# A layer chain on one core: the attention stage reordered into whole steps of two heads

## Chip, cores, metric

One Trainium2 chip, one of its cores. The kernel is one program in Bass with the Tile framework: the order of TensorE's instructions (PE) is the order in which the Python code issues them, while the orders of VectorE (DVE), ScalarE (ACT), GpSimd (POOL) and of the DMA queue on SyncE (SP) are set by Tile's scheduler, from the priorities that the code gives. Every engine then works through its own list strictly in that order and waits on semaphores. The metric is the time on the device in microseconds, a median over runs.

## What is computed

Two layers over 256 latent tokens and 256 context tokens of width 1024. Each layer is a half-step SwiGLU, a mixer (layer 0: neighbourhood attention, layer 1: a short gated convolution), and a second SwiGLU, each with an adaptive modulation and a LayerNorm. The stage that matters here is the attention of layer 0, with 16 heads of 64:

```python
qkv = (hx @ w_qkv).reshape(B, S, 3, N_HEADS, HEAD_DIM)
q = apply_axial_rope(qkv[:, :, 0], rope)
k = apply_axial_rope(qkv[:, :, 1], rope)
...
s_win = jnp.einsum('bjqhd,bjkhd->bhjqk', q_r, k_blk).astype(jnp.float32) * scale
s_win = jnp.where(mask, s_win + bias.astype(jnp.float32)[None], -jnp.inf)
s_ctx = jnp.einsum('bjqhd,bchd->bhjqc', q_r, k_c).astype(jnp.float32) * scale
p = jax.nn.softmax(jnp.concatenate([s_win, s_ctx], axis=-1), axis=-1).astype(v.dtype)
return (jnp.einsum('bhjqk,bjkhd->bjqhd', p[..., :nk], v_blk)
        + jnp.einsum('bhjqc,bchd->bjqhd', p[..., nk:], v_c))
...
y_lat = jnp.moveaxis(o, 0, 1).reshape(B, S, D) @ w_out
```

With 256 latent tokens in four grid rows, every query sees 256 latent keys (the window is a mask) and 256 context keys: 512 keys in all, four key tiles of 128.

## The kernel before

Everything is fp32, done as products of two parts: each operand is split into a high part `hi` (a copy by ACT) and a low part `lo` (a subtraction by DVE), and a product is hi·hi + hi·lo + lo·hi. So one pass over the contraction costs three matmuls, and whatever goes through TensorE is first touched once by ACT and once by DVE (`split`, lines 104-106).

**Weights.** `wunit` loads 256 rows by 512 columns by DMA (L175), then ACT makes `hi` in two halves (L178) and DVE `lo` in two halves (L181). There are four raw buffers, five for `hi` and five for `lo`; a buffer comes free when the last matmul that reads it is done.

**Chunks.** A chunk is the work on one token tile with one weight unit: six matmuls of 128x512 (L156, L157, L159). `tile_panel` makes a panel of four chunks for one token tile and hands the PSUM bank to `each`: for keys and values (`kv_quarter`, 256 columns of K and 256 of V, i.e. four heads), DVE applies the rotary factors to K (`roped`, L708 to L715; for context tokens ACT copies, L760) and `split` writes V. `q_half` makes Q for eight heads. After its panels, `rest` transposes K or Q on TensorE (kT, L773; qT, L791), and `split` makes the high and low parts. This `rest` is a `Late`: it runs when `tick`, called after every chunk, has counted its delay (1 chunk for kT, 2 for qT), or at once when somebody asks for it with `get()`.

**The attention pipeline.** `scores(h, qt)` takes two heads and one of the two query tiles: six matmuls S of 64x512 (L814) into two banks, then per head the bias (DVE L818), the maximum (DVE L820), the exponential (ACT L822), the reciprocal (DVE L823) and the scaling (ACT L824). `probs_T` transposes one head's 128x512 probabilities in four TensorE transposes (PT, L836) and splits them (ACT L105, DVE L106). When both query tiles of a head are there, `values(h)` multiplies with V: eight matmuls o of 128x256 (L848, L849), whose halves are added up (ACT L854, DVE L855) and, after the second head of a pair, split into `oT`. The loop runs over half-steps i, one head and query tile each: S of two heads at every even i, PT of one head two half-steps later (`A_LAG`), o of one head one half-step after that (`V_LAG`). Between them TensorE gets chunks from `fill`, at a rate per half-step (`R0` to `R3`): first the other quarters of K and V and the second half of Q (`filler`, 56 chunks), and from i = 24 on the first nine chunks of the output projection wo (`last_filler`), which need `oT`.

**PSUM.** Eight banks: three with tag `mm` (panels, o, two of wo's accumulators), three with tag `at` (S, and wo's third accumulator), two with tag `tp` (all transposes). Wo's accumulators are held from their first chunk until the attention is over, so that from then on one `mm` bank is left for o.

After the loop come the other wo chunks, the LayerNorm, and the next SwiGLU, whose weights are loaded ahead.

Of the kernel before, what the change touches and what calls it, by code (L numbers as in the profile page):

```python
# [35 lines left out]
LEAD = 5  # L36
TAIL = 3
XAT = 1
A_LAG = 2
A_PRE = 2  # L40
NX_AT = 2
R0 = 2.4
R1 = 2.9
R2 = 1.9
R3 = 1.0
LN_LAG = (5, 5)
LT_LAG = (5, 5)
F0_LAG = (5, 5, 6, 7)
G_LAG = 4
ROPE_EARLY = 70  # L50
S_EARLY = 40
V_LAG = 1
AHEAD = 3
P_EARLY = 70
V_EARLY = 70
W_HI = 2
# [8 lines left out]
def backbone_kernel(  # L65
# [315 lines left out]
    def run(gen):  # L381
        for _ in gen:
            pass
# [336 lines left out]
    def bias_pair(h, qt):  # L720


        for hh in (h, h + 1):
            bt = hp.tile([P, 4, 64], F32, tag="bias", bufs=4, name=nm("bias"))
            for i in range(2):
                bias_dma[:] = [sync.dma_start(bt[64 * i:64 * i + 64],
                                              bass.AP(na_rpb_rev.tensor,
                                                      na_rpb_rev.offset + hh * 465 + (7 - 2 * qt - i) * 31 - 48,
                                                      [[1, 64], [31, 4], [1, 64]]))]
            nc.gpsimd.tensor_tensor(out=bt, in0=bt, in1=win_sb[:, ::-1].unsqueeze(1).to_broadcast([P, 4, 64]),  # L730
                                    op=ALU.add)
            BIAS[hh, qt] = bt[:, :, ::-1]
# [71 lines left out]
    def scores(h, qt):  # L804

        ch = h % 8 // 2
        qh, ql = Q[h // 8].get()[ch // 2]
        qs = slice((ch % 2) * 256 + qt * P, (ch % 2) * 256 + (qt + 1) * P)
        kh, kl = KV[h // 4][0].get()[(h % 4) // 2]
        banks = [bank("at", "S") for _ in range(2)]  # L810
        for f in range(3):
            for i in range(2):
                ps = slice(64 * i, 64 * i + 64)
                nc.tensor.matmul(banks[i], (qh, qh, ql)[f][ps, qs], (kh, kl, kh)[f][ps, :], start=f == 0, stop=f == 2)  # L814
        res = []
        for i, S in enumerate(banks):
            Sv = S[:, 0:256].rearrange("p (a b) -> p a b", a=4)
            nc.vector.tensor_tensor(out=Sv, in0=Sv, in1=BIAS.pop((h + i, qt)), op=ALU.add)  # L818
            mx = hp.tile([P, 3], F32, tag="mx", bufs=6, name=nm("mx"))
            nc.vector.tensor_reduce(out=mx[:, 0:1], in_=S, axis=AX.X, op=ALU.max, negate=True)  # L820
            pr = hp.tile([P, 512], F32, tag="pr", bufs=4, name=nm("pr"))
            nc.scalar.activation(pr, S, AF.Exp, bias=mx[:, 0:1], accum_out=mx[:, 1:2])  # L822
            nc.vector.reciprocal(mx[:, 2:3], mx[:, 1:2])  # L823
            nc.scalar.activation(pr, pr, AF.Copy, scale=mx[:, 2:3])  # L824
            res.append(pr)
        return res
# [3 lines left out]
    def probs_T(h, qt, pr):  # L830
        if h not in PT:
            PT[h] = [hp.tile([P, 4, 256], F32R, tag="pt", bufs=4, name=nm("pT")) for _ in range(2)]
        pth, ptl = PT[h]
        pt = tpb("PT")
        for k in range(4):
            nc.tensor.transpose(pt[:, k * P:(k + 1) * P], pr[:, k * P:(k + 1) * P], ident)  # L836
        split(pt.rearrange("p (k q) -> p k q", k=4), pth[:, :, qt * P:(qt + 1) * P], ptl[:, :, qt * P:(qt + 1) * P])
# [3 lines left out]
    def values(h):  # L841

        pth, ptl = PT.pop(h)
        ps = mmb("o")[:, 0:256]
        s = slice(h % 4 * P, (h % 4 + 1) * P)
        v = KV[h // 4][1]
        for k in range(4):
            nc.tensor.matmul(ps, v[k][:, s], pth[:, k], start=k == 0, stop=False)  # L848
            nc.tensor.matmul(ps, v[k][:, s], ptl[:, k], start=False, stop=k == 3)  # L849
        if h % 2 == 0:  # L850
            osum[0] = sp.tile([P, 512], F32, tag="tmp", bufs=3, name=nm("osum"))[:, 0:256]
        p0 = h % 2 * 64
        t = osum[0][p0:p0 + 64]
        nc.scalar.activation(t, ps[64:128], AF.Copy)  # L854
        nc.vector.tensor_tensor(out=t, in0=ps[0:64], in1=t, op=ALU.add)  # L855
        if h % 2:
            if len(oT) <= h // 4:
                oT.append([hp.tile([P, 512], F32R, tag="oT", bufs=6, name=nm("oT")) if len(oT) < 3 else act(F32R, "oT")
                           for _ in range(2)])
            cs = slice((h // 2 % 2) * 256, (h // 2 % 2) * 256 + 256)  # L860
            split(osum[0], *(z[:, cs] for z in oT[h // 4]))
# [15 lines left out]
    def last_filler():  # L877
        with tc.issue_after(bias_dma[-1].ins):
            for t in range(2):
                for h in range(2):  # L880
                    xt[t][h] = act(F32, "x")
                    sync.dma_start(xt[t][h], xscr[t * P:(t + 1) * P, h * 512:(h + 1) * 512])
            gen, nh, lt = sub_end(na_w_out[0], lhs_T(oT), KC, 0, 1, 5, 1.0, (0, 6), "wo", order_late(KU))
        box.extend([nh, lt])
        yield from gen

    box = []
    fill = filler()
    rate = [R0] * 8 + [R1] * 8 + [R2] * 8 + [R3] * 12
    credit = 0.0  # L890
    steps = [(h + i, qt) for h in range(0, NH, 2) for qt in range(2) for i in range(2)]
    prs = {}
    LAG = A_LAG
    fin = None

    def fill_some(n):
        for _ in range(n):
            if next(fill, 0) == 0:
                break

    fill_some(A_PRE)
    for i in range(len(steps) + LAG + V_LAG):
        if i == NX_AT:
            new_x(0, 0, s2t)
            for t in range(2):
                for h in range(2):
                    sync.dma_start(xscr[t * P:(t + 1) * P, h * 512:(h + 1) * 512], xt[t][h])
        while i + AHEAD < len(steps) and len(KV) <= steps[i + AHEAD][0] // 4:
            fill_some(1)
        if i < len(steps) and i % 2 == 0:  # L910
            with tc.high_priority(offset=S_EARLY):
                prs[i], prs[i + 1] = scores(*steps[i])
            if i % 2 == 0 and i + 2 < len(steps):
                bias_pair(*steps[i + 2])
        credit += rate[min(i, len(rate) - 1)]
        n = int(credit)
        credit -= n
        if i >= 24 and fin is None:
            run(fill)
            fin = last_filler()  # L920
            fill = islice(fin, 9)
        fill_some((n + 1) // 2)
        if 0 <= i - LAG < len(steps):
            with tc.high_priority(offset=P_EARLY):
                probs_T(*steps[i - LAG], prs.pop(i - LAG))
        fill_some(n // 2)
        j = i - LAG - V_LAG
        if j >= 0 and steps[j][1] == 1:
            with tc.high_priority(offset=V_EARLY):
                values(steps[j][0])  # L930
    run(fill)
    run(fin)
    phase.__exit__(None, None, None)
# [129 lines left out]
```

## Time and profile before

| | us |
|---|---|
| median of 3 runs | 1285.99 (1285.16, 1285.99, 1287.23) |
| the profiled execution, its time | 1289.17 |
| its span in the profile | 1287.4 |
| attention loop, first S to last o | 441.8 to 589.3 |
| PE busy, whole span | 1257.7 (98%) |
| DVE / ACT busy, whole span | 955.1 (74%) / 591.2 (46%) |

The time of the profiled execution is 1.8 us more than its span. How to read the rows that follow: in the timeline a row has its start in us from the span's start, its length in us, the engine, the line, the operation, what it writes and reads, and the count where equal rows were merged; in brackets the time that the engine sat idle before it, and what ended the wait. In a view of stretches a row has the stretch, its length, and for PE, PEld (weight loads), DVE, ACT and POOL the busy time with the number of instructions, then TensorE's granted clock (1 is full), the share of the DMA engines' time, and GB/s. A matmul's length contains its way through the pipeline, so the time that one costs in a row of them is the distance between two starts.

### The profile page before, as it was taken

Reading aid. Unit: us, or ns where it says so; the run is one execution under the profiler, and the core shown is the slowest. Engines: PE = TensorE matmul, PEld = TensorE weight load, DVE = VectorE, ACT = ScalarE, POOL = GpSimd, SP = SyncE. Lnnn points to the kernel's source line nnn. Section 1 sums busy time; section 2 is a strip of 40 time slices with the busy share of each in tenths; the row PEclk is TensorE's granted clock in tenths of the full one; section 3 lists DMA queues with packets and bytes.
Section 4 is the critical chain, followed back from the end, with each engine's and each line's share of the span. In section 5 each row is a group of like instructions: output and inputs, shape, how many; then the busy total and the mean of one; then the engine's idle time right before and its main releaser. Section 6 shows DMA issues by size and latency. Waiting matters only on the chain.

```text
span 1287.4 us, 17193 instructions
## 1 busy us (share of the span) xinstructions
PE 1257.7 (98%) x5890; PEld 1007.0 (78%) x5890; DVE 955.1 (74%) x1683; ACT 591.2 (46%) x1148; POOL 42.0 (3%) x71
## 2 busy tenths in 40 slices
PE   7999999999999999988999999999999999999997
PEld 4787778788778877766887787887787877788886
DVE  3699877485658777788998787757778788855545
ACT  2432132413236456686555435654435645655431
POOL 0000000000001111110000000000000000000000
PEclk9999999999999999999999999999999999999999
DMA  9977569484622744464999887666887764666641
GB/s 284 299 231 243 181 193 297 131 297 146 198 78 76 215 91 92 90 147 149 305 331 328 295 294 262 215 215 225 289 287 241 215 211 147 210 217 185 231 155 51
DMA packets 202712, 268.59 MB, mean 209 GB/s; under 512 B 30026, under 2 KB 149298, under 8 KB 202624
## 3 DMA queue, kind: packets, MB, share of 16 engines
q1 hardware_dynamic: 202624, 267.49, 65.9%
q8 instruction: 46, 0.75, 0.2%
q14 instruction: 42, 0.34, 0.1%
HBM read 265.27 MB, written 2.17 MB: 208 GB/s over the span
## 4 chain that ended last, share of the span: by engine, by line
PE 78%; DVE 8%; DMA 8%; ACT 3%; issue 2%; SPq 1%; POOL 0%; DVEq 0%; ACTq 0%
PE w L156 13%; PE w L157 13%; PE w L159 13%; PE f L541 6%; PE f L542 6%; PE f L543 6%; DMA ar<-in_ada_w_dram 5%; DMA w1r<-in_ffn_w_in_dram 2%; PE wkv L156 2%; PE wkv L157 2%; PE wkv L159 2%; PE wc L156 2%; PE wc L157 2%; PE wc L159 2%; DVE w1l L181 2%
## 5 line engine op out<-in xcount | busy, mean ns | idle before, releaser
L178 ACT ACTIVATE w1h<-w1r 128x512 fp32r<-128x512 f32 x352 | 203.3, 626 | 185.0 <-PE w L159 75.4
L181 DVE TENSOR_TENSOR w1l<-w1r,w1h 128x512 fp32r<-128x512 f32 x352 | 227.6, 684 | 66.5 <-ACT w1h L178 64.3
L156 PE MATMUL w<-w1h,hTh 128*128 128x512 f32 x528 | 211.6, 401 | 3.8 <-ACT hTh L105 3.7
L247 DVE SCALAR_TENSOR_TENSOR acc<-ar,cst,acc 128x512 f32<-128x512 f32 x266 | 187.2, 745 | 34.8 <-DMA ar<-in_ada_w_dram 34.8
L157 PE MATMUL w<-w1l,hTh 128*128 128x512 f32 x528 | 207.7, 393 | 0.0
L156 PE MATMUL w<-w2h,gh 128*128 128x512 f32 (+1 forms) x446 | 175.4, 394 | 0.0
L157 PE MATMUL w<-w2l,gh 128*128 128x512 f32 (+1 forms) x446 | 173.7, 390 | 0.3 <-DVE w2l L181 0.3
L178 ACT ACTIVATE w2h<-w2r 128x512 fp32r<-128x512 f32 x176 | 101.5, 624 | 140.9 <-PE w L159 131.6
L159 PE MATMUL w<-w1h,hTl 128*128 128x512 f32 x528 | 163.9, 392 | 0.6 <-DVE hTl L106 0.6
L181 DVE TENSOR_TENSOR w2l<-w2r,w2h 128x512 fp32r<-128x512 f32 x176 | 114.0, 686 | 43.5 <-ACT w2h L178 42.3
L541 PE MATMUL f<-h0h,w1h 128*128 128x512 f32 x352 | 139.8, 397 | 0.4 <-ACT w1h L178 0.4
L542 PE MATMUL f<-h0h,w1l 128*128 128x512 f32 x352 | 138.4, 393 | 0.0
L543 PE MATMUL f<-h0l,w1h 128*128 128x512 f32 x352 | 138.3, 393 | 0.0
L159 PE MATMUL w<-w2h,gl 128*128 128x512 f32 (+1 forms) x446 | 136.3, 387 | 0.0
L156 PEld LDWEIGHTS w<-w1h,hTh 128*128 128x128 f32 x528 | 99.5, 188 | 28.2 <-ACT hTh L105 5.5
L159 PEld LDWEIGHTS w<-w1h,hTl 128*128 128x128 f32 x528 | 99.5, 189 | 24.1 <-DVE hTl L106 1.4
L157 PEld LDWEIGHTS w<-w1l,hTh 128*128 128x128 f32 x528 | 99.6, 189 | 20.4 <-DVE w1l L181 0.3
L156 PEld LDWEIGHTS w<-w2h,gh 128*128 128x128 f32 x446 | 83.7, 188 | 21.7 <-issue 1.7
L157 PEld LDWEIGHTS w<-w2l,gh 128*128 128x128 f32 x446 | 83.8, 188 | 18.6 <-DVE w2l L181 1.3
L159 PEld LDWEIGHTS w<-w2h,gl 128*128 128x128 f32 x446 | 83.3, 188 | 18.7
L541 PEld LDWEIGHTS f<-h0h,w1h 128*128 128x128 f32 x352 | 66.6, 189 | 18.4 <-issue 3.7
L543 PEld LDWEIGHTS f<-h0l,w1h 128*128 128x128 f32 x352 | 66.5, 189 | 14.7 <-DVE h0l L519 0.3
(178 smaller groups left out, 1702.5 us busy)
## 6 DMA issues: line engine op xcount, KB each, us to landing
w1r<-in_ffn_w_in_dram SPq DMA_DIRECT2D x352, 256.0 KB
ar<-in_ada_w_dram SPq DMA_DIRECT2D x128, 512.0 KB
w2r<-in_ffn_w_out_dram SPq DMA_DIRECT2D x88, 512.0 KB
ar<-in_ada_w_dram SPq DMA_DIRECT2D x32, 256.0 KB
wkvr<-in_na_w_qkv_dram SPq DMA_DIRECT2D x32, 256.0 KB
wcr<-in_sc_w_in_dram SPq DMA_DIRECT2D x32, 256.0 KB
wqr<-in_na_w_qkv_dram SPq DMA_DIRECT2D x8, 512.0 KB
bias<-in_na_rpb_dram SPq DMA_DIRECT2D x64, 64.0 KB
```

Of the source, the lines that this page charges most:

```text
L156: nc.tensor.matmul(ps, lh, rh, start=first and i == 0, stop=False)
L157: nc.tensor.matmul(ps, lh, rl, start=False, stop=False)
L159: nc.tensor.matmul(ps, ll, rh, start=False, stop=last and i == n - 1)
L178: nc.scalar.activation(hi[:, a:a + m // W_HI], raw[:, a:a + m // W_HI], AF.Copy)
L181: nc.vector.tensor_tensor(out=lo[:, a:b], in0=raw[:, a:b], in1=hi[:, a:b].bitcast(F32), op=ALU.subtract)
L247: nc.vector.scalar_tensor_tensor(out=a, in0=src, scalar=sc, in1=a, op0=ALU.mult, op1=ALU.add)
L541: nc.tensor.matmul(ps, lh, hT0[k][0], start=(k == 0), stop=False)
L542: nc.tensor.matmul(ps, ll, hT0[k][0], start=False, stop=False)
L543: nc.tensor.matmul(ps, lh, hT0[k][1], start=False, stop=(k == KC - 1))
```

## The change

```diff
-A_LAG = 2
 A_PRE = 2
-NX_AT = 2
-R0 = 2.4
-R1 = 2.9
-R2 = 1.9
-R3 = 1.0
+NX_AT = 1
+W_FROM = 11
+R0 = 5.0
+R1 = 4.8
+R2 = 4.0
+R3 = [2, 1, 2, 1, 2]
...
-V_LAG = 1
-AHEAD = 3
...
-    rate = [R0] * 8 + [R1] * 8 + [R2] * 8 + [R3] * 12
+    steps = [(h, qt) for h in range(0, NH, 2) for qt in range(2)]
+    rate = [R0] * 4 + [R1] * 4 + [R2] * 3 + [3] + R3
     credit = 0.0
-    steps = [(h + i, qt) for h in range(0, NH, 2) for qt in range(2) for i in range(2)]
     prs = {}
-    LAG = A_LAG
     fin = None
...
-    for i in range(len(steps) + LAG + V_LAG):
+    for i in range(len(steps) + 1):
...
-        while i + AHEAD < len(steps) and len(KV) <= steps[i + AHEAD][0] // 4:
-            fill_some(1)
-        if i < len(steps) and i % 2 == 0:
+        if i < len(steps):
             with tc.high_priority(offset=S_EARLY):
-                prs[i], prs[i + 1] = scores(*steps[i])
-            if i % 2 == 0 and i + 2 < len(steps):
-                bias_pair(*steps[i + 2])
-        credit += rate[min(i, len(rate) - 1)]
+                prs[i] = scores(*steps[i])
+            if i + 1 < len(steps):
+                bias_pair(*steps[i + 1])
+        credit += rate[i]
         n = int(credit)
         credit -= n
-        if i >= 24 and fin is None:
+        fill_some((n + 1) // 2)
+        while i + 1 < len(steps) and len(KV) <= steps[i + 1][0] // 4:
+            fill_some(1)
+        if i:
+            h, qt = steps[i - 1]
+            with tc.high_priority(offset=P_EARLY):
+                for z, pr in enumerate(prs.pop(i - 1)):
+                    probs_T(h + z, qt, pr)
+        if i == W_FROM:
             run(fill)
+            settle()
             fin = last_filler()
             fill = islice(fin, 9)
-        fill_some((n + 1) // 2)
-        if 0 <= i - LAG < len(steps):
-            with tc.high_priority(offset=P_EARLY):
-                probs_T(*steps[i - LAG], prs.pop(i - LAG))
         fill_some(n // 2)
-        j = i - LAG - V_LAG
-        if j >= 0 and steps[j][1] == 1:
+        if i and qt == 1:
             with tc.high_priority(offset=V_EARLY):
-                values(steps[j][0])
+                values(h)
+                values(h + 1)
```

A step i is now two heads and one query tile: S of both, half of the step's chunks, PT of both heads of the step before, the other half of the chunks, and, after every second step, o of both heads. The 56 chunks of `filler` last until step 11 of 16; there `settle()` runs every waiting `Late`, so kT of the last quarter follows at once, and wo's nine chunks are spread over steps 11 to 16. Every engine has the same instructions as before; what differs is their order, and only within the attention stage, on TensorE from the chunks ahead of the second S on. Because the file is two lines shorter above the loop, lines 57 to 884 of the old file are 55 to 882 of the new.

Three places of the order are shown. The first is TensorE before S of heads 8 and 9, the first that reads Q's second half (qr is that Q after the rotary factors, two token tiles; qT its transposes). Before, with S of heads 6 and 7 ahead of the transposes and chunks of K and V behind them:

```order
L814 MATMUL S_4598<-kTh_4048,qTl_3565 128x512
L814 MATMUL S_4599<-kTh_4048,qTl_3565 128x512
L791 MATMUL qT_4628<-ident,qr_4474 128x128
L791 MATMUL qT_4628<-ident,qr_4542 128x128
...
L791 MATMUL qT_4637<-ident,qr_4474 128x128
L791 MATMUL qT_4637<-ident,qr_4542 128x128
L156 MATMUL wkv_4548<-wkvh_4647,hTh_3268 128x512
L157 MATMUL wkv_4548<-wkvl_4648,hTh_3268 128x512
```

Now:

```order
L157 MATMUL wkv_4630<-wkvh_4632,hTl_3255 128x512 x2
L789 MATMUL qT_4646<-ident,qr_4518 128x128
L789 MATMUL qT_4646<-ident,qr_4624 128x128
...
L789 MATMUL qT_4655<-ident,qr_4518 128x128
L789 MATMUL qT_4655<-ident,qr_4624 128x128
L812 MATMUL S_4664<-kTh_4449,qTh_4651 128x512
L812 MATMUL S_4665<-kTh_4449,qTh_4651 128x512
```

`scores` asks for Q when only one chunk has gone by since Q's last panel, so the transposes come one chunk after that panel, where there had been two chunks, an o and an S; and S of heads 8 and 9 stands directly behind them, where there had been chunks.

The second place is TensorE where the last quarter's K is transposed. Before, one PT ahead of kT, and S behind it:

```order
L849 MATMUL o_5024<-pT_4910,v_4365 128x256
L836 MATMUL PT_5041<-ident,pr_4936 128x128 x4
L773 MATMUL kT_5048<-ident,kr_4676 128x128
...
L773 MATMUL kT_5057<-ident,kr_4676 128x128
...
L814 MATMUL S_5066<-kTh_5053,qTh_4642 128x512
```

Now:

```order
L157 MATMUL wkv_4943<-wkvh_4739,hTl_3494 128x512 x2
L834 MATMUL PT_5032<-ident,pr_4887 128x128 x4
L834 MATMUL PT_5041<-ident,pr_4894 128x128 x4
L771 MATMUL kT_5048<-ident,kr_4753 128x128
...
L771 MATMUL kT_5057<-ident,kr_4753 128x128
...
L154 MATMUL wo_5091<-woh_5084,oT_4064 128x512
```

kT now stands right behind the last chunk of its own quarter and the two PT of a step, and a wo chunk stands between it and S of heads 12 and 13.

The third place is ACT around the o of heads 12 and 13 (osum<-o empties the bank of an o, woh casts a weight of wo, pr are exponentials and scalings of the next step). Before:

```order
L854 ACTIVATE osum_5324<-o_5315 64x256
L824 ACTIVATE pr_5276<-pr_5276,mx_5274 128x512
L178 ACTIVATE woh_5395<-wor_5394 128x512
L178 ACTIVATE woh_5463<-wor_5462 128x512 x2
L822 ACTIVATE pr_5338,mx_5336<-S_5327,mx_5336 128x512
L105 ACTIVATE pT_5370<-PT_5372 128x4x128
L822 ACTIVATE pr_5345,mx_5343<-S_5328,mx_5343 128x512
L854 ACTIVATE osum_5324<-o_5379 64x256
```

Now:

```order
L822 ACTIVATE pr_5269<-pr_5269,mx_5267 128x512
L852 ACTIVATE osum_5324<-o_5315 64x256
L820 ACTIVATE pr_5276,mx_5274<-S_5259,mx_5274 128x512
L176 ACTIVATE woh_5463<-wor_5462 128x512
L822 ACTIVATE pr_5276<-pr_5276,mx_5274 128x512
L852 ACTIVATE osum_5324<-o_5327 64x256
```

Before, seven other instructions of ACT and a chunk of TensorE lay between the two osum, and the o of head 13 came later than that of head 12 by as much. Now both o stand in a row on TensorE, and the osum of head 12 stands behind a scaling of the next step.

## The prediction

> **What bounds the kernel now.** I read the page's slices first, 32.2 us each: PE is busy for nine tenths or more nearly everywhere; the two that show 8 inside the program are the 18th and 19th, 547 to 611 us. Next came stretches of 20 us through the attention, 441.8 to 589.3 us; after the length each row has the busy time of PE, PEld, DVE, ACT, POOL.
>
> ```profile
> PE   7999999999999999988999999999999999999997
> ...
> 460.00:480.00 20.00, 19.83 (x106) 16.21 (x105) 15.08 (x30) 13.74 (x31) 1.93 (x2) 1.00 0.54 124
> ...
> 520.00:540.00 20.00, 19.84 (x106) 15.58 (x105) 13.94 (x34) 10.49 (x24) 2.94 (x4) 1.00 0.38 77
> 540.00:560.00 20.00, 16.74 (x97) 12.40 (x96) 17.43 (x38) 18.58 (x41) 3.52 (x4) 0.94 0.56 94
> 560.00:580.00 20.00, 19.50 (x114) 15.40 (x113) 15.67 (x35) 15.42 (x33) 4.94 (x6) 0.97 0.61 160
> 580.00:605.00 25.00, 20.92 (x105) 16.01 (x105) 20.25 (x41) 15.97 (x35) 1.61 (x3) 1.00 0.38 110
> ```
>
> Up to 540 us TensorE leaves out 0.17 us in one of these stretches, 0.16 in another: it is the bound, and no order of the same instructions makes that part shorter. From 540 on it waits, and ACT, with 18.58 of 20 us, is full. The timeline of PE has the waits one by one, in brackets:
>
> ```profile
> 549.02 0.39 PE L848 MATMUL o<-pT,v 128*128 128x256 f32 x1 [0.74 <-ACT pT L105]
> ...
> 549.97 0.39 PE L849 MATMUL o<-pT,v 128*128 128x256 f32 x1 [0.56 <-DVE pT L106]
> ...
> 554.35 0.66 PE L773 MATMUL kT<-ident,kr 128*128 128x128 f32 x4 [0.41 <-DVE pT L106]
> ...
> 556.55 0.66 PE L773 MATMUL kT<-ident,kr 128*128 128x128 f32 x4 [1.55 <-DVE pT L106]
> ...
> 575.69 0.38 PE L849 MATMUL o<-pT,v 128*128 128x256 f32 x1 [0.50 <-DVE pT L106]
> ...
> 585.03 0.66 PE L836 MATMUL PT<-ident,pr 128*128 128x128 f32 x4 [0.54 <-DVE pT L106]
> ...
> 586.23 0.39 PE L849 MATMUL o<-pT,v 128*128 128x256 f32 x1 [0.42 <-DVE pT L106]
> ...
> 588.24 0.38 PE L848 MATMUL o<-pT,v 128*128 128x256 f32 x1 [0.92 <-DVE osum L855]
> ...
> 590.83 0.50 PE L156 MATMUL wo<-woh,oT 128*128 128x512 f32 x1 [0.90 <-ACT oT L105]
> ```
>
> Their sum is 6.54 us; the 0.33 before 540 make it 6.9. The clock was halved too (the number before the last two), in one stretch here and in one much later:
>
> ```profile
> 547.50:550.90 3.40, 2.10 (x16) 1.62 (x13) 3.40 (x8) 3.40 (x10) 0.00 (x0) 1.00 0.61 143
> ...
> 554.30:557.70 3.40, 1.80 (x12) 1.18 (x14) 3.00 (x8) 3.37 (x9) 0.74 (x1) 1.00 0.92 190
> 557.70:561.10 3.40, 3.40 (x10) 2.26 (x11) 3.40 (x7) 1.25 (x3) 0.93 (x2) 0.50 0.41 58
> ...
> 796.70:800.10 3.40, 0.69 (x4) 0.61 (x4) 1.40 (x3) 3.40 (x10) 0.00 (x0) 1.00 1.05 341
> 800.10:803.50 3.40, 3.40 (x10) 2.62 (x9) 3.30 (x7) 3.40 (x7) 0.00 (x0) 0.50 0.11 35
> ```
>
> After a stretch with PE busy for 1.80 of 3.4 us, or for 0.69, the next 3.4 us ran at 0.50: half of its work was lost, 1.7 us. After 2.10 it was not. So the attention has 6.9 + 1.7 = 8.6 us to win, 0.7% of the time; all else in the change can only add.
>
> **The change part by part.** First the work of TensorE itself, from distances between starts:
>
> ```profile
> 461.58 0.39 PE L156 MATMUL wkv<-wkvh,hTh 128*128 128x512 f32 x1
> ...
> 462.94 0.39 PE L156 MATMUL wkv<-wkvh,hTh 128*128 128x512 f32 x1
> ...
> 534.88 0.60 PE L836 MATMUL PT<-ident,pr 128*128 128x128 f32 x4
> 535.24 0.47 PE L156 MATMUL wkv<-wkvh,hTh 128*128 128x512 f32 x1
> ...
> 541.98 0.28 PE L848 MATMUL o<-pT,v 128*128 128x256 f32 x1
> ...
> 542.93 0.40 PE L156 MATMUL wkv<-wkvh,hTh 128*128 128x512 f32 x1
> ```
>
> A chunk costs 1.36 us, a PT 0.36 (and 0.08 on the first matmul after it), an o 0.95. Two PT or two o in a row cost twice that within 0.02 us, the instructions are the same, and so are the six of an S. That term is 0: cover is not needed, since TensorE issues all of it either way. The bias DMAs and POOL's additions keep their place of one step ahead, and the four stores of x go out in the same step as before; both lie a whole step (some 8 us of TensorE) ahead of use. What is left is waits.
>
> *Q's second half.* The last panel of Q has to go through DVE before qT (rows of PE, then DVE, then ACT):
>
> ```profile
> 512.22 0.61 PE L159 MATMUL wq<-wqh,hTl 128*128 128x512 f32 x2
> ...
> 517.79 1.09 PE L791 MATMUL qT<-ident,qr 128*128 128x128 f32 x8
> ...
> 513.34 0.68 DVE L708 TENSOR_TENSOR qr<-wq,rope 128x512 f32<-128x512 f32 x1
> ...
> 515.20 0.68 DVE L715 TENSOR_TENSOR qr<-qr,r 128x512 f32<-128x512 f32 x1
> ...
> 518.48 0.60 ACT L105 ACTIVATE qTh<-qT 128x512 fp32r<-128x512 f32 x1 [1.10 <-PE qT L791]
> ```
>
> From the panel's last matmul (512.83) to the rotated Q (515.88) it is 3.05 us, with a cast and two rotary products between the two rows. TensorE came for it 4.96 us after the panel. Now one chunk lies between, 1.36 us, so TensorE waits up to 3.05 - 1.36 = 1.7 us; DVE's list has a PT split where the cast was, as long. Then S of heads 8 and 9 directly behind: qT's start to the end of qTh is 518.48 + 0.60 - 517.79 = 1.3 us, TensorE is there after 0.9, which leaves 0.4. I take 2.0. Below: 0.4, if DVE has caught up; above: 3.5, with two casts of ACT (0.62 each) ahead of qTh. While it waits, S's chain and all chunks behind are late by as much.
>
> *The last kT.* Transposes have two banks, and both PT of the step before now fill them directly ahead of kT. How long a bank stays taken, where nothing else queues:
>
> ```profile
> 535.52 0.60 ACT L105 ACTIVATE pT<-PT 128x512 fp32r<-128x512 f32 x1 [0.39 <-PE PT L836]
> ...
> 536.15 0.69 DVE L106 TENSOR_TENSOR pT<-PT,pT 128x512 fp32r<-128x512 f32 x1 [2.04 <-ACT pT L105]
> ```
>
> PT started at 534.88, the bank is free at 536.84: 1.96 us. The first kT comes 0.8 us after the first PT, so it waits at least 1.1 us, and the second bank comes 0.6 us after the first against 0.4 of transposes: 1.3 in all. But kT's own quarter has just ended: ACT has a copy and a V split of it ahead of the PT (0.38 each), and between the two PT one cast of wo, as DVE has:
>
> ```profile
> L178 ACT ACTIVATE woh<-wor 128x512 fp32r<-128x512 f32 x16 | 9.5, 623 | 0.4 <-PE wo L159 0.4
> ...
> L181 DVE TENSOR_TENSOR wol<-wor,woh 128x512 fp32r<-128x512 f32 x16 | 10.9, 687 | 0.9 <-ACT woh L178 0.9
> ```
>
> With 0.3 us for the copy and the split (they start while PT runs) and one cast of 0.6, it is 2.2; between 1.3 and 3.8 (ACT and DVE both behind by another two casts). It takes the place of 0.41 + 1.55 = 1.96. So kT is sooner, and no better off: before, it waited for one PT's bank, now for two. The S behind it no longer waits, nor did it.
>
> *o in pairs.* While wo's accumulators are held, one bank is left for o, and the second o of a pair waits until the first is emptied. Before, that was so once, at the end: 588.24, 0.92 us with both engines idle:
>
> ```profile
> 587.36 0.38 ACT L854 ACTIVATE osum<-o 64x256 f32<-64x256 f32 x1 [1.04 <-PE o L849]
> ...
> 587.77 0.42 DVE L855 TENSOR_TENSOR osum<-o,osum 64x256 f32<-64x256 f32 x1 [0.40 <-ACT osum L854]
> ```
>
> Now it is so for heads 11, 13 and 15. For 11 and 13 osum stands behind a scaling of ACT (0.72) which is partly over by then: 1.1 and 1.6, together 2.7. For 15 two casts of wo stand ahead of it, which wait for the wo chunk just before: 0.92 + 0.4 = 1.3. Sum 4.0, between 2.8 (all at 0.92) and 6.0 (a scaling, an exponential and a cast ahead of each). In the earlier stage three banks serve panels and o, and o comes 2 x 1.36 us after the PT against 1.96 + 0.6 us for both splits: nothing.
>
> *PT of the last step.* From S of heads 14 and 15 to their probabilities:
>
> ```profile
> 576.71 0.50 PE L814 MATMUL S<-kTh,qTh 64*128 64x512 f32 x2
> ...
> 577.61 0.24 PE L297 MATMUL mcT<-ident,mrow 32*128 32x32 f32 x1
> ...
> 582.92 0.71 ACT L824 ACTIVATE pr<-pr,mx 128x512 f32<-128x512 f32 x1
> ```
>
> It is 6.9 us. TensorE now has in between an S (0.9), the small mcT (0.2), two chunks and a pair of PT, 4.7 with the 0.08 behind transposes: up to 2.2 us of wait. Three casts of wo that stood in ACT's list there before are gone from it: I take 0.8, from 0 to 2.2. The last wait, wo for oT (0.90), stays.
>
> *What goes away.* The waits of o at 549 and 575.69 and 586.23 (2.2 us together), of PT at 585.03 (0.54), and the 0.3 before 540.
>
> *Sum of waits:* 2.0 + 2.2 + 4.0 + 0.8 + 0.9 = 9.9 against 6.9: +3.0. The rest of the program starts from the last o, its queue is behind it, and it has no slack to lose or to give: PE is busy throughout, so 1 us here is 1 us at the end.
>
> *The clock.* It was halved after 1.80 of 3.4 us busy. The stretch at the new kT (two PT, 1.1 and more of waiting, eight kT, a wait in between) has some 1.6 of 3.4, the one at qT 1.7. The second halving in the program lies 242.4 us behind the first, 71 times 3.41, so the stretches may stand on a fixed grid, and whether a gap fills one is then chance, about one half each. I take one halving, as in the trace before: 0.
>
> [...]
>
> So the profiled execution's 1289.17 becomes 1289.17 + 3.0 = 1292.2. The runs' median lies 3.2 below the profiled one, and the change is the same there: 1285.99 + 3.0 = **1289.0**. A measurement of this kernel can tell 0.2% (2.6 us) from no change, and the forecast lies just beyond.
>
> **The rivals.**
>
> *A wash.* PT and o pairs give ACT and DVE longer runs of equal work, the lists are shorter where TensorE comes for them, and the new waits are at their lower bounds: 0.4 + 1.3 + 2.8 + 0 + 0.9 = 5.4 against 6.9, or halfway to the forecast's, 7.6. For it: DVE has 13.9 of 20 us in the middle. Against it: the bank of o is one, whatever the queues do. Time 1284.5 to 1287.9, where the forecast's range begins.
>
> *Faster.* The tail is what ACT's list makes of it: 18.58 of 20 us in 540 to 560, with four casts of wo in a row on the way to PT. Filler now lasts to step 11 and one S, two PT and two o are done before the last chunk; if ACT is thereby ahead for good, the waits at kT fall to 0.5, those of o to 0.92 each, and the clock stays up: 0.4 + 0.5 + 2.8 + 0 + 0.9 = 4.6, so 4.6 - 6.9 - 1.7 = -4.0: 1282. Against it: what is done earlier is done by the same TensorE, and the casts stand between the two PT.
>
> *Both stretches halve the clock.* A halving more than before costs 1.7; with waits halfway to the upper bounds (3.5 + 3.8 + 6.0 + 2.2 + 0.9 = 16.4; halfway 13.1) it is 13.1 - 6.9 + 1.7 = +7.9: 1293.9, and 1291.5 at least. It decides once less than about 1.8 us of 3.4 is busy at qT as well as at kT.
>
> **How the numbers follow.** The forecast, +1.9 to +5.5, has 0.45: it needs only the bank of o and the qT. The worse case has 0.12, the wash 0.21, faster 0.20; 0.02 is anything else. Slower by over 0.2% means above 1288.6: 0.52 (0.38 of the forecast's, the worse case, and a little of the rest). Within: 0.28. Faster, below 1283.4: 0.20. The forecast's own range is 1287.9 to 1291.5; with half of either outer case, 1282.0 to 1293.0.
>
> **What would show it.** In the timeline of PE after: a wait ahead of qT and S for heads 8 and 9 of 1.5 to 2.5 us, where there was none; waits ahead of both kT, together about 2, ended by DVE's pT split; the second o of the pairs 10/11, 12/13 and 14/15 waiting for osum, 0.9 to 1.6 each; one halving or two near them. The stretch up to 540 us should have 2 us less of PE than now. I am wrong if the second o does not wait, if qT is there in time, or if TensorE is still full up to step 11 and the waits after it come to less than 6 us.

## The result and the profile after

| | before | changed |
|---|---|---|
| median of 12 runs each, side by side | 1286.5 us (1283.1 to 1290.6) | 1290.7 us (1289.5 to 1295.0) |
| ratio changed / before | | 1.0041, 95% interval 1.0028 to 1.0053 |
| the profiled execution, time / span | 1289.17 / 1287.4 us | 1289.49 / 1287.7 us |
| first S of the attention to the first hT behind it (hT: the transposes ahead of the next SwiGLU), in the trace | 441.83 to 599.09: 157.3 us | 440.57 to 603.93: 163.4 us |
| clock halvings in that stretch (a granted clock of 0.50 for 3.4 us) | 1 | 2 |

The change makes the kernel slower by 0.41%, 5.3 us by the ratio and 4.2 us between the medians. The two profiled executions alone would have hidden it: their spans differ by 0.3 us. The stage in which the order was changed shows it, 6.1 us.

The stretches of the changed kernel (the columns are those of the rows of before):

```profile
480.00:500.00 20.00, 20.00 (x108) 16.12 (x107) 13.89 (x31) 13.54 (x31) 4.47 (x5) 1.00 0.35 56
500.00:520.00 20.00, 17.32 (x96) 13.81 (x94) 16.10 (x34) 14.29 (x31) 4.04 (x4) 1.00 0.62 131
520.00:540.00 20.00, 19.25 (x106) 15.05 (x107) 16.29 (x37) 10.60 (x23) 2.32 (x3) 1.00 0.48 106
540.00:560.00 20.00, 18.04 (x94) 14.32 (x93) 14.89 (x32) 14.90 (x33) 4.51 (x5) 0.94 0.46 90
560.00:580.00 20.00, 16.81 (x98) 13.23 (x98) 14.41 (x32) 13.57 (x31) 2.92 (x4) 0.98 0.59 150
580.00:605.00 25.00, 21.72 (x108) 16.60 (x108) 16.71 (x36) 13.63 (x28) 1.62 (x3) 0.93 0.23 66
```

Before, TensorE was full up to 540 us; now it leaves out 2.68 us between 500 and 520 and 0.75 between 520 and 540. From 540 to 560 it is busier than before (18.04 against 16.74), and ACT is no longer full there: 14.90 us, 18.58 before. From 560 to 580 it is less busy, 16.81 against 19.50. So the even spread of the chunks relieved ACT. What it cost shows in the timeline of PE, whose waits of over 0.5 us up to 600 us are all here:

```profile
504.04 0.66 PE L834 MATMUL PT<-ident,pr 128*128 128x128 f32 x4 [0.89 <-DVE kTl L104]
...
520.50 0.98 PE L789 MATMUL qT<-ident,qr 128*128 128x128 f32 x7 [2.18 <-DVE qr L713]
521.73 0.50 PE L812 MATMUL S<-kTh,qTh 64*128 64x512 f32 x2 [0.25 <-ACT qTh L103]
...
555.77 0.66 PE L771 MATMUL kT<-ident,kr 128*128 128x128 f32 x4 [1.42 <-DVE pT L104]
556.97 0.68 PE L771 MATMUL kT<-ident,kr 128*128 128x128 f32 x4 [0.54 <-DVE pT L104]
...
567.43 0.39 PE L846 MATMUL o<-pT,v 128*128 128x256 f32 x1 [1.20 <-DVE osum L853]
...
579.79 0.39 PE L846 MATMUL o<-pT,v 128*128 128x256 f32 x1 [1.80 <-DVE osum L853]
...
588.05 1.27 PE L834 MATMUL PT<-ident,pr 128*128 128x128 f32 x8 [0.61 <-ACT pr L822]
593.08 0.38 PE L846 MATMUL o<-pT,v 128*128 128x256 f32 x1 [1.42 <-DVE osum L853]
595.66 0.50 PE L154 MATMUL wo<-woh,oT 128*128 128x512 f32 x1 [0.90 <-ACT oT L103]
```

They sum to 11.2 us, with the row of S; before, the rows from 549 us on summed to 6.54. All were forecast but the first: a PT at 504 us that waits for DVE to empty a bank of kT. Then the clock:

```profile
516.50:519.90 3.40, 1.82 (x9) 1.20 (x7) 3.40 (x7) 3.15 (x7) 1.47 (x2) 1.00 0.62 167
519.90:523.30 3.40, 2.55 (x15) 1.60 (x16) 3.28 (x6) 1.09 (x2) 0.00 (x0) 1.00 0.26 70
554.10:557.50 3.40, 1.44 (x12) 0.97 (x11) 2.90 (x6) 3.40 (x9) 1.46 (x2) 1.00 0.42 52
557.50:560.90 3.40, 3.40 (x12) 2.27 (x12) 3.01 (x6) 1.60 (x4) 0.60 (x1) 0.50 0.82 290
578.00:581.40 3.40, 1.60 (x12) 1.43 (x14) 2.59 (x6) 3.32 (x8) 0.26 (x1) 1.00 0.39 120
581.40:584.80 3.40, 3.40 (x13) 2.20 (x10) 2.85 (x7) 1.29 (x4) 0.00 (x0) 0.50 0.60 186
```

The stretches are laid in steps of 3.4 us from the start of a halving, which lasts 3.41 us in the trace (581.37 to 584.78). It was halved twice: after the stretch with kT's waits (1.44 of 3.4 us busy) and after the one with the wait for osum ahead of the o of head 13 (1.60). The wait at qT, the longest of all, was cut in two by the edge between the first two rows (1.82 and 2.55 us busy), and no halving followed it. In the second halving two 128x512 matmuls of wo start 0.43 us apart (583.45 and 583.88), behind it 0.23 (586.35 and 586.58). The granted clock is 0.50 for 3.4 us, so a halving counts as 1.7 us here, an estimate. By starts the waits cost 4.4 us more than before (163.4 - 2 x 1.7 against 157.3 - 1.7), the second halving 1.7; together the 6.1.

Why do the spans not show it? The changed kernel's execution came to the attention 1.3 us sooner, and in the SwiGLU near 800 us, which the change does not touch, it waited 0.89 us where the other waited 2.71, with a halving behind it that the changed one did not have:

```profile
802.16 0.50 PE L154 MATMUL w<-w1h,hTh 128*128 128x512 f32 x1 [0.89 <-ACT hTh L103]
```

Before:

```profile
799.41 0.50 PE L156 MATMUL w<-w1h,hTh 128*128 128x512 f32 x1 [2.71 <-ACT hTh L105]
```

Both can come to either kernel, as the next section shows.

### The profile page after: what moved, and what is told of

Its sections match the earlier page's. It is cut to its first block, busy times and chain, and to the rows that moved or that the text cites. A ratio compares the mean times of both kernels' runs of the same rounds, so it can differ in the third digit from the quotient of the medians.

```text
span 1287.7 us, 17190 instructions
## 1 busy us (share of the span) xinstructions
PE 1255.0 (97%) x5890; PEld 1005.9 (78%) x5890; DVE 954.2 (74%) x1683; ACT 590.6 (46%) x1148; POOL 43.6 (3%) x71
## 4 chain that ended last, share of the span: by engine, by line
PE 89%; DVE 4%; ACT 3%; DMA 3%; issue 1%; POOL 0%; SPq 0%; DVEq 0%; ACTq 0%
PE w L154 17%; PE w L155 17%; PE w L157 17%; PE f L539 6%; PE f L540 6%; PE f L541 6%; PE wkv L154 2%; PE wkv L155 2%; PE wkv L157 2%; PE wc L154 2%; PE wc L155 2%; PE wc L157 2%; DMA w1r<-in_ffn_w_in_dram 2%; PE gT L398 1%; PE S L812 1%; PE ada L263 1%
```

## The experiments

Each is the changed kernel with one edit, unless said otherwise. The column of the attention is measured from S of the second step to the first hT behind the attention, since the very first S waits up to 0.4 us in some traces (0.39 in e5_kt); "net" takes 1.7 us off for each halving, and the last column is the ratio of the runs to those of the kernel before beside them, with its interval. Each experiment has one trace, so how far its attention varies by itself is not known. The expectations take waits from the distance between starts, which gives up to 0.16 us more than the profile's brackets, the measure of the text.

| | attention | halvings | net | against the changed kernel | ratio of the runs |
|---|---|---|---|---|---|
| changed kernel, both traces | 155.4 | 2 | 152.0 | | 1.0041 (1.0028 to 1.0053) |
| e1_q | 154.0 | 2 | 150.6 | -1.5 | 1.0013 (1.0000 to 1.0026) |
| f1_q3 | 152.5 | 1 | 150.8 | -1.2 | 1.0029 (1.0015 to 1.0043) |
| e4_kv2 | 154.5 | 2 | 151.1 | -1.0 | 1.0035 (1.0022 to 1.0049) |
| e5_kt | 153.6 | 1 | 151.9 | -0.2 | 1.0040 (1.0025 to 1.0055) |
| e2_obank | 154.6 | 3 | 149.5 | -2.5 | 1.0022 (1.0007 to 1.0037) |
| f2_ob_mc | 152.2 | 1 | 150.5 | -1.6 | 1.0025 (1.0011 to 1.0039) |
| f3_all | 149.9 | 1 | 148.2 | -3.8 | 1.0004 (0.9990 to 1.0018) |
| g1_swap | 149.6 | 1 | 147.9 | -4.1 | 1.0002 (0.9990 to 1.0015) |

**The same kernels again.** The changed one:

> The changed kernel again, as it is, for a second trace. If the two halvings of the clock in the attention come from the order alone, both are there again, at the wait ahead of kT and at the wait ahead of o of head 13. If they hang on where a fixed grid of 3.413 us falls on the waits, one or both are gone or stand elsewhere, and the attention is shorter by 1.7 us for each that is gone, while the waits themselves stay (5 of over 1 us ahead of PT, qT, kT and o) within 0.2 us each. Also open: the stretch near 800 us, where the kernel before had a wait of 2.86 us and a halving and the changed one 1.05 us and none. If that differs by chance too, this run may show it with the changed kernel.

It took 1292.1 us, ratio 1.0046 (1.0025 to 1.0067). All waits of the attention are there again, none off by more than 0.03 us, and from the first S to the first hT it is 163.4 us as before (441.17 to 604.53). But the halvings moved:

```profile
519.60:523.00 3.40, 1.58 (x11) 1.05 (x11) 3.34 (x7) 1.81 (x4) 0.11 (x1) 1.00 0.20 67
523.00:526.40 3.40, 3.40 (x10) 2.36 (x9) 3.06 (x7) 0.74 (x2) 0.00 (x0) 0.50 0.49 143
557.10:560.50 3.40, 2.05 (x12) 1.67 (x13) 3.34 (x6) 3.40 (x8) 2.13 (x2) 1.00 0.32 82
560.50:563.90 3.40, 3.40 (x19) 2.26 (x18) 3.40 (x8) 0.74 (x2) 0.00 (x0) 1.00 0.95 307
577.60:581.00 3.40, 1.61 (x13) 1.40 (x12) 2.97 (x7) 3.35 (x9) 0.73 (x1) 1.00 0.17 39
581.00:584.40 3.40, 3.40 (x14) 2.32 (x13) 1.70 (x4) 1.55 (x4) 0.00 (x0) 0.50 0.82 251
```

This time the wait at qT lay inside one stretch (1.58 us busy) and a halving followed, while the same waits at kT were split over two (2.05 in the second) and none did; at head 13 it was halved again (1.61). So the order alone does not settle which waits are followed by a halving: the waits were the same in both traces, and what differed was how they lay in the stretches. The changed order has five waits of 1 us and more and was hit twice in both traces; the kernel before has one or two and was hit once in both of its traces. That more long waits are hit oftener fits these four traces, and is not shown beyond them. The halving near 800 us was there too (at 802.9; the matmul that starts at 802.75 takes 0.71 us, where the first trace has 0.50), so it belongs to neither kernel. And the kernel before:

> The kernel before, as it is, for a second trace of it. The changed kernel's two traces agree to 0.01 us in the attention. If the same holds here, the stretch from the first S of the attention to the first hT behind it is 157.3 us again, or 155.6 if the halving at kT falls away with the grid; what differs between the two traces then lies at the start and near 800 us. Rival: the attention before varies by itself by 1 us or more, and part of the 6.1 us between the two kernels' traces is chance.

It took 1284.4 us, ratio 0.9990 (0.9979 to 1.0001) to itself. Here my theory fell. The attention was 159.3 us (440.88 to 600.17), 2.0 more than in the first trace at an equal number of halvings, one, now behind 572 to 576 us. DVE and PE there:

```profile
572.51 0.43 DVE L818 TENSOR_TENSOR S<-S,bias 128x256 f32<-128x256 f32 x1 [1.20 <-POOL bias L730]
```

```profile
575.47 0.44 PE L849 MATMUL o<-pT,v 128*128 128x256 f32 x1 [2.02 <-DVE pT L106]
```

S waited for its bias, which POOL had just got by DMA (its addition starts at 571.74 us, released by that DMA); a split of P^T stands behind it in DVE's list, and o behind that: 2.02 us where the first trace had 0.50. So the kernel before differs by 2 us in the attention between its two traces, the changed one by 0.01. The difference of the kernels is between 4.1 us (163.4 - 159.3) and 6.1; half-way, 5.1, is near the 5.3 of the ratio, on two traces each.

**Q's second half.**

```diff
+        if i == 8:
+            fill_some(2)
         if i < len(steps):
...
-        fill_some((n + 1) // 2)
+        if i != 8:
+            fill_some((n + 1) // 2)
```

> Two chunks moved ahead of S of heads 8 and 9, that is, ahead of the transposes of Q's second half (the first half of step 8's chunks; nothing added). My theory: these transposes come one chunk (1.36 us) after the last panel of Q and wait for the rotary work of DVE, 2.34 us in the trace, and S waits 0.28 us behind them. With three chunks between, 4.1 us against 3.7 of DVE, both waits are gone: 2.6 us less in the attention, 0.2% less time. Rival: DVE is behind as a whole, its PT splits come between, and qT waits on for 1 us or more, or the wait turns up at the next PT: less than 1 us won.

The delay of qT is two chunks at most, so only one more came between, not two. The wait fell by 1.17 us, about that chunk:

```profile
520.97 0.98 PE L789 MATMUL qT<-ident,qr 128*128 128x128 f32 x7 [1.01 <-DVE qr L713]
```

DVE gave the rotated Q when it would have given it anyway. The attention is 1.5 us shorter, the runs 3.6 by the ratios. The rest may be the clock: the mean clock of the runs is 0.9970 against 0.9952, an estimate of 2.3 us (0.0018 x 1290). But f1_q3, below, takes the wait at qT away altogether and has runs only 1.5 us shorter by the ratios, at a mean clock of 0.9958. So what the wait at qT costs in halvings is not shown. The wait's reason stands in DVE's list of the changed kernel:

```profile
516.82 1.17 DVE L179 TENSOR_TENSOR wkvl<-wkvr,wkvh 128x512 fp32r<-128x512 f32 x1
517.90 0.68 DVE L706 TENSOR_TENSOR qr<-wq,rope 128x512 f32<-128x512 f32 x1
518.51 0.74 DVE L711 TENSOR_TENSOR r<-wq,rope 128x256 f32<-128x256 f32 x2
519.17 0.67 DVE L104 TENSOR_TENSOR pT<-PT,pT 128x512 fp32r<-128x512 f32 x1
519.77 0.67 DVE L713 TENSOR_TENSOR qr<-qr,r 128x512 f32<-128x512 f32 x1
```

A cast of 1.17 us stands ahead of the first product, where the list of before has one of 0.69, and a split of P^T ahead of the last. Why this cast is so long is open: POOL's addition of a bias starts 0.13 us ahead of it (516.69), and no run tests whether that matters. Two more chunks ahead of qT, and one between qT and S:

```diff
-        res.append(Late(2, rest))
+        res.append(Late(2 + g, rest))
...
+        if i == 8:
+            fill_some(3)
...
-        fill_some(n // 2)
+        fill_some(n // 2 - (i == 8))
```

(with the first half of step 8 left out as in e1_q)

> As e1_q, but with three chunks between Q's last panel and its transposes, and one more chunk between these and S of heads 8 and 9. In e1_q one chunk more took the wait ahead of qT from 2.34 to 1.0 us, since DVE gave the rotated Q at the same time as before. My theory: DVE's time is set by what stood in its list before (a split of P^T, the products, two casts) and not by TensorE, so another chunk takes the last 1.0 us and the 0.28 us ahead of S: 2.4 to 2.6 us less in the attention than the changed kernel, no stretch near 520 us of under 1.9 us of TensorE. Rival: the casts for the added chunk go ahead of the rotary work in DVE's list and push it back by 0.7 us, so that 0.5 us or more of wait is left.

The rival was right that over 0.5 us is left, but not in its way: the rotary work is not pushed back. qT no longer waits; the third chunk does, for the low part of its weights, which DVE makes behind the rotary work:

```profile
521.91 0.50 PE L155 MATMUL wkv<-wkvl,hTh 128*128 128x512 f32 x1 [0.85 <-DVE wkvl L179]
```

So 0.85 of the 2.4 us is DVE's own lateness, and here it went to the next place where TensorE needs DVE.

**The wait that was not forecast.**

```diff
-        res.append((Late(1, rest), v))
+        res.append((Late(3 if g == 2 else 1, rest), v))
```

> The transposes of K of the third quarter come three chunks after its end where they came one chunk after it. My theory for the wait of 1.05 us ahead of PT at 504 us (0.27 ahead of the other), which I had not foreseen: kT of that quarter stands one chunk ahead of a pair of PT, the four of them share two banks, and DVE has both of kT's banks to empty. With two chunks more between, if PT goes ahead of kT or well behind it, the wait is gone: 1.0 to 1.3 us less. Rival: kT now stands directly behind the pair of PT, or directly ahead of S, and waits itself, as it does in the last quarter (2.0 us): no gain, or up to 1 us lost.

The net is 1.0 us, but not all from that place. PT waits no more there, and kT itself waits 0.31 us behind the pair of PT and a chunk, so 0.6 of the 0.89 us is won. Another 0.46 comes from qT, which waits 1.72 us here in place of 2.18:

```profile
504.61 1.25 PE L771 MATMUL kT<-ident,kr 128*128 128x128 f32 x8 [0.31 <-DVE pT L104]
...
519.83 0.98 PE L789 MATMUL qT<-ident,qr 128*128 128x128 f32 x7 [1.72 <-DVE qr L713]
```

That kT stood so near to the pair of PT, with two banks for all transposes, was the cause of the wait at 504 us. In the runs the ratio is 0.06% less, which drowns in the intervals.

**The last kT.**

```diff
-        fill_some((n + 1) // 2)
+        if i != W_FROM + 1:
+            fill_some((n + 1) // 2)
...
-            settle()
             fin = last_filler()
...
-        fill_some(n // 2)
+        fill_some(n // 2 + (i == W_FROM))
```

> The transposes of the last quarter's K between two chunks of wo: no settle() there, one chunk of wo more ahead of S of heads 12 and 13, one less behind. My theory: kT waits 2.0 to 2.2 us only because the two PT directly ahead fill both transposing banks; a chunk of 1.36 us between takes 1.3 us of it at least, and 0.3 to 0.9 us are left. Rival: the chunk of wo needs casts of ACT and DVE that stand ahead of the splits of P^T, so TensorE waits for the cast or the bank as long as before, less than 0.5 us won.

The wait went as my theory has it, from 1.96 us (1.42 and 0.54) to one of 0.55:

```profile
559.68 0.66 PE L771 MATMUL kT<-ident,kr 128*128 128x128 f32 x4 [0.55 <-DVE pT L104]
```

Yet the attention won 0.2 us net and the runs nothing. With PT starts as marks, it was 1.2 us ahead of the changed kernel behind kT and lost most of that again in the next three steps. My reading is that TensorE was sooner there, and ACT and DVE were not.

**The bank of o.** Both heads of a pair go into the halves of one bank, and are emptied behind the second:

```diff
-        pth, ptl = PT.pop(h)
-        ps = mmb("o")[:, 0:256]
+        bk = mmb("o")
...
+        for z in range(2):
+            pth, ptl = PT.pop(h + z)
+            ps = bk[:, z * 256:(z + 1) * 256]
...
             with tc.high_priority(offset=V_EARLY):
                 values(h)
-                values(h + 1)
```

> Both o of a pair go into the two halves of one bank and are emptied after the second. My theory: the second o of the pairs 10/11, 12/13 and 14/15 waits (1.36, 1.96 and 1.58 us in the trace) because one bank is left and has to be emptied in between; with one bank for both, none of the three waits is there, 4.9 us less, and the halving of the clock behind the o of head 13 has nothing to come from, 1.7 us less: about 6.6 us in the attention, less what the last pair gives back, because wo's next bank then waits for both to be emptied (about 0.5 us more ahead of the last wo). Rival: the casts of wo's weights and ACT's scalings are what is late, o only shows it; then the wait moves to the next wo, PT or S, and less than 3 us are won.

The waits of PE for the attention, one line for each pair of waiter and releaser, with the sum, the count and the longest:

```profile
PE PT L834 <- DVE pT L104: 2.1, 1, 2.1
PE kT L771 <- DVE pT L104: 1.9, 2, 1.4
PE wo L154 <- ACT oT L103: 1.8, 1, 1.8
```

The three waits for osum, 4.42 us, are gone, so the one bank was their cause. But 2.1 us of wait turned up at a PT of the last steps where there had been 0.61, another 0.8 at a wo, and the last wo waits 1.8, not 0.9, since both heads are now emptied behind the last o. Net 2.5 us are won, less than the 3 of the rival, and some 0.6 of that at Q, whose waits are 1.8 in all here (perhaps because the banks of the panels fall otherwise, which was not tested). So the rival is right as far as the worth goes: most of the wait moved. And the halving did not go: one came behind the new wait at PT (matmuls of wo start 0.43 us apart from 585.82 on), and one more behind that of the last wo (0.43 from 594.93 on). I took the wait at PT for the bank that mcT held:

```diff
-        return Late(6, rest)
+        return Late(mc_late[0], rest)
```

(`mc_late[0]` is 10 for wo, 6 elsewhere)

> As e2_obank, and the small transpose mcT four chunks later, behind the last o, where it had stood ahead of the last pairs of PT. In e2_obank the three waits for osum were gone, but PT of heads 14 and 15 then waited 2.06 us at 584.5 us. My theory: mcT holds one of the two transposing banks until DVE copies it at 585.4 us, so the second PT waits for the only other bank; with mcT later this wait shrinks to the scaling of the probabilities, 0.5 us or less, and 1.5 to 2 us more than in e2_obank are won, about 4.6 to 5 us against the changed kernel in the attention. Rival: ACT's scaling of the second head is what PT waits for (it ends 0.4 us before that PT starts); then mcT's move wins 0.4 us at most.

```profile
PE PT L836 <- ACT pr L824: 2.3, 1, 2.3
...
PE wo L154 <- ACT oT L103: 1.8, 1, 1.8
```

With mcT out of the way the same PT waits 2.3 us for the scaling of its probabilities: my theory fell, the rival holds. Nothing was won (net 150.5 us after 149.5). The chain of softmax of the last steps, on DVE and ACT, is what ends there.

**All at once**: the edits of f1_q3, e4_kv2, e5_kt and f2_ob_mc, with the two copies of ACT ahead of the two additions of DVE:

```diff
         for z in range(2):
+            nc.scalar.activation(osum[0][z * 64:z * 64 + 64], bk[64:128, z * 256:(z + 1) * 256], AF.Copy)
+        for z in range(2):
             ps = bk[:, z * 256:(z + 1) * 256]
             t = osum[0][z * 64:z * 64 + 64]
-            nc.scalar.activation(t, ps[64:128], AF.Copy)
             nc.vector.tensor_tensor(out=t, in0=ps[0:64], in1=t, op=ALU.add)
```

> All of it at once: three chunks ahead of Q's transposes, K of the third quarter three chunks after its end, the last K between two chunks of wo, both o of a pair in one bank with both copies of ACT ahead of both additions of DVE, mcT behind the last o. If the waits are what I take them for, they go down from about 12.8 us to about 4 (the last wo 1.5, rests elsewhere), and both halvings lose what sets them off: the attention is 8 to 11 us shorter than in the changed kernel and about 3 us shorter than before, 1282 to 1284 us. Rival: the work of ACT and DVE in the last four steps is the limit, a wait taken away comes back at the next PT or wo; then 4 to 6 us, and no faster than before.

1287.1 us, the time of the kernel before (1286.9), as the rival had it. The attention is 5.6 us shorter, 3.8 net. The waits left:

```profile
PE PT L836 <- ACT pr L824: 2.4, 2, 1.3
PE wo L154 <- ACT oT L103: 1.7, 1, 1.7
PE kT L773 <- DVE pT L104: 1.5, 2, 1.1
...
PE wo L154 <- ACT pr L822: 0.9, 1, 0.9
```

The last try was f3_all with S of the next step ahead of the two o (the last pair of o behind the loop):

```diff
             with tc.high_priority(offset=S_EARLY):
                 prs[i] = scores(*steps[i])
+        if late_o:
+            with tc.high_priority(offset=V_EARLY):
+                values(late_o.pop())
...
-                values(h)
+            late_o.append(h)
```

> As f3_all, and S of the next step ahead of the two o, not behind them. In f3_all what is left of the waits is 2.4 us ahead of the last PT, ended by ACT's scaling of the probabilities, and 1.7 us ahead of the last wo. My theory: the chain from the last S (DVE's bias and maximum behind two osum and casts, exponential, scaling) sets PT's time; S 1.9 us earlier takes 1.5 to 2 us of these waits, and 1 us of the waits ahead of S and wo near 567 us: 1284 to 1285.5 us, faster than before by 0.1 to 0.2%. Rival: o is later by an S, osum and oT with it, and the splits of P^T and casts fill ACT and DVE as before; then less than 1 us is won and the time is that of f3_all.

1287.1 us again (1285.7 for the kernel before beside it, ratio 1.0002), as the rival had it. The wait of PT for ACT's scaling is gone, and others have its place:

```profile
PE kT L773 <- DVE pT L104: 1.9, 3, 1.2
PE wo L154 <- ACT oT L103: 1.7, 1, 1.7
PE S L814 <- ACT pr L822: 1.4, 2, 1.2
PE PT L836 <- DVE pT L104: 1.0, 2, 0.6
```

So the whole-step order can be mended to the time of the kernel before, within the intervals; no version measured beats it.

## Why the prediction was right, and where it was not

Forecast 1289.0 us, measured 1290.7; slower by over 0.2%, as the likeliest case had it. As a difference, +3.0 us were forecast, and +4.2 (medians) to +5.3 (ratio) measured. The sum of the forecast, term by term, the waits by the profile's brackets:

| term | forecast | measured |
|---|---|---|
| Q's second half: qT, and S behind it | 2.0 | 2.18 + 0.25 = 2.4 |
| last kT | 2.2 | 1.42 + 0.54 = 2.0 |
| o in pairs, heads 11, 13, 15 | 1.1 + 1.6 + 1.3 = 4.0 | 1.20 + 1.80 + 1.42 = 4.4 |
| PT of the last step | 0.8 | 0.61 |
| last wo | 0.9 | 0.90 |
| PT of step 6, behind the third quarter's kT | none | 0.89 |
| sum of the waits (before: 6.9) | 9.9 | 11.2 |
| halvings beyond before's one | 0 | 1 in both traces, 1.7 |

**What held.** The bound: TensorE is full or waits, and its own work did not change. The places of the waits that were named, their releasers, and their sizes within 0.5 us each. f1_q3, e2_obank and e5_kt, each by changing its cause, show that the causes were those named: DVE's rotary work, the single bank, and the two PT in the transposing banks. They also show that a wait is not worth its length: of 2.4, 4.4 and 2.0 us, 1.2, 2.5 and 0.2 were won net. That kT is no better off also held (2.0 us in both kernels). It came sooner only in the order, a chunk ahead of the S that needs it; in time it started later, at 555.77 us against 554.35.

**What failed: "I take one halving, as in the trace before: 0".** That was the largest error of a single term, 1.7 us in the traces. For the runs it is 1.4, an estimate from the mean clock of the 12 runs (0.9952) and of 26 runs of before (0.9963). The prediction looked for candidates at kT and qT and left out its own term of o: the wait for osum ahead of the o of head 13 was followed by a halving in both traces, with 1.60 and 1.61 us busy. With the waits as measured, 11.2 - 6.9 = 4.3, and one halving more, the sum is +6.0, near the 6.1 of the first traces. That the runs show less, 4.2 to 5.3, fits the 1.5 us more that the kernel before waited at an o in its second trace: the forecast counted the waits of before from a good execution. So two errors of opposite sign were in it, and that the time landed inside the range owes something to luck. The rival that had two halvings was right in their number, with other places and smaller waits. It asked for less than about 1.8 us busy at qT as well as at kT: it was 1.82 and 1.44 us in the first trace, 1.58 and 2.05 in the second, and each time only the smaller was followed by one.

**What was missed:** the two transposing banks were counted for the last quarter, and not for the third, whose kT comes one chunk ahead of a pair of PT: 0.89 us, and e4_kv2 takes it away. In Q's term the rotated Q was reckoned 3.05 us behind the panel's last matmul, and came after 3.6 (516.82 to 520.44). The split of P^T stands "where the cast was", as forecast; most of the rest is the cast ahead of the first product, 1.17 us and not 0.69.

**"1 us here is 1 us at the end"** holds for the runs (5.1 us halfway between the traces of the attention, 5.3 by the ratio), and not for a single pair of traces, where the start and the stretch at 800 us made up for most of the 6.1. The statement that the bias lies a whole step ahead of its use holds for the changed kernel's two traces, and not always for the kernel before: in its second trace the bias was 1.2 us late. It was no part of the sum, but makes the gain of the old order smaller than its first trace said.

**Where the halvings fell.** The prediction gave each of its two places one half. In the changed kernel's two traces qT and kT were followed by a halving once each, and the o of head 13, which it had not named for this, both times. f1_q3 has both outcomes in one trace, the stretch at kT and the one at head 13, each with the stretch behind it:

```profile
551.90:555.30 3.40, 1.98 (x14) 1.58 (x13) 1.74 (x5) 3.40 (x10) 0.15 (x1) 1.00 0.52 61
555.30:558.70 3.40, 2.86 (x18) 2.03 (x18) 3.40 (x7) 3.07 (x6) 1.92 (x2) 1.00 0.55 171
575.80:579.20 3.40, 1.60 (x12) 1.42 (x14) 2.60 (x6) 3.33 (x8) 0.27 (x1) 1.00 0.39 125
579.20:582.60 3.40, 3.40 (x13) 2.20 (x10) 2.84 (x7) 1.27 (x4) 0.00 (x0) 0.50 0.56 183
```

In the first stretch 1.98 us were busy, of which 0.84 were chunks and the rest transposes, and the clock stayed at 1.00; in the third 1.60 us were busy, and it fell to 0.50.

## What to carry to other kernels

An order that puts like work side by side (two PT, two o, S behind its own transposes) makes each pair meet its banks at once (here 4.4 us of waits at o and 2.0 at kT): count the banks at every such place, not only where the trace already shows a wait. Where TensorE was otherwise full, waits of 1.6 to 2.0 us within one stretch of 3.4 us were followed by a halved clock in both traces of either kernel (another 1.7 us each by the estimate above), though not each time (1.7 us at 591.6 in the changed one were not), so look at how much waiting falls close together, and not only at the sum. And two profiled executions do not show a difference of 0.4%; the changed stage, measured between two fixed instructions in more than one trace, does. A wait with a proven cause can still be worth little: what stood behind it on the other engines may be as late as before.

## What the hardware showed besides

In three traces two halvings begin a whole multiple of 3.41 us, the length of one, apart: in the changed kernel's first at 557.47 and 581.37 (7 times), in its second at 523.0 and 581.0 (17 times), in the first of before at 557.73 and 800.08 (71 times). That fits the grid of the prediction, on these three distances. With the stretches laid in these steps, those ahead of a halving had 0.69 us of TensorE (before, near 800 us), 1.38 (its second trace), 1.44 to 1.61 (the changed kernel and f1_q3), 1.80 (before, at kT) and 2.2 (g1_swap, 3.4 less a wait of 1.17). Others were passed without one at 1.75 and 1.82 us (the changed kernel's first trace, 591.6 to 595.0 and 516.5 to 519.9), 1.98 (f1_q3), 2.05 (the changed kernel's second trace) and 2.10 (before). So the busy time alone does not tell in these traces which stretch is followed by one.

The clock goes with a part of the spread of the runs. Over the 84 runs of before beside the experiments, the median is 1290.1 us for the five with a mean clock of 0.994, 1287.7 for the 14 with 0.995, 1285.8 for the 36 with 0.997, and 1285.2 for the six with 0.998. Single runs fall out of that line, 1283.0 us at 0.994 and 1289.1 at 0.999, so it is not the only source.
